# Routing stage of a two-layer diffusion transformer: which rows are transposed token-major, and where norm factor, scale and shift are applied

## The chip, the cores and the metric

The kernel runs on one core of one Trainium2 chip. The metric is the device time of one execution in microseconds (us). Five engines appear in the profile: PE (TensorE; PEld is its weight load), DVE (VectorE), ACT (ScalarE), POOL (GpSimd) and SP (SyncE), which here issues the loads of the weights.

## The reference, cut to what matters

256 tokens of width 1024 pass through two layers. The second layer ends in a mixture of experts; `norm_ffn_g`, `sc2` and `sh2` are rows of 1024.

```python
hl = rms_norm(xl, norm_ffn_g[1]) * (1 + sc2) + sh2     # rms_norm: x * rsqrt(mean(x*x) + eps) * g
xl = xl + g2 * moe_swiglu(hl, router, w1, w3, w2)

def moe_swiglu(h, router, w1, w3, w2):
    vals, idx = lax.top_k((h @ router).astype(jnp.float32), 2)
    wts = jax.nn.softmax(vals, axis=-1)
    combine = jnp.sum(jax.nn.one_hot(idx, 8) * wts[..., None], axis=-2)
    for e in range(8):
        y = y + combine[..., e:e + 1] * ((jax.nn.silu(h @ w1[e]) * (h @ w3[e])) @ w2[e])
```

With `A = (1 + sc2) * norm_ffn_g` per feature and `r` per token, a row of `hl` is `x * r * A + sh2`.

## The kernel before, in words

**Layout.** The residual lies feature-major: `xt[k]`, k from 0 to 7, holds features 128k to 128k+127 on its partitions and the 256 tokens in its first 256 columns; the other 256 columns are free by the routing stage. `r` lies token-major, two columns for two tiles of 128 tokens.

**Experts.** Only tokens that picked an expert are computed. For an expert, a one-hot matrix (token by slot) is multiplied with a token-major copy of the normed rows, `htok` (256 tokens by 1024), which yields `xg`: the expert's rows, feature-major, in up to 128 slots. Four experts ("large", positions 0, 2, 4, 6 of the list `SEQ`) run with 128 slots and an accurate product of three matmuls: `mm3` (L261 to L263) multiplies hi by hi, hi by lo and lo by hi, where hi is the rounded value and lo the remainder. The other four ("small") have 64 slots and one plain product; their rows are gathered at once by `gather_small` into the free half of `xt`. Expert 0 comes first; the order of the others is worked out on the chip from the counts (`order_a`), and SP loads the resulting indices into its registers (`order_load`, L1411) before it may issue any load of the other seven.

**Weights.** All weights come as pieces of 1 MB through ten buffers (`raw` and `q`, five each). For a large expert ACT makes hi of a piece (L233) and DVE lo (L211), into three pairs of hi and lo tiles, and the buffer is then free for the next load. Small experts multiply straight from the buffer. Large and small experts alternate in steps: hidden products (`eh`, `eh_small` L1538), transposes of the hidden rows (`et` L1558), output products (`ey`, `ey_small` L1595), and after an expert's last step `scatter` (L1618, L1622).

**Order.** Each engine works in the order in which the program names its instructions; nothing reorders them. A large expert's `gather` stands behind `ey` of the large expert before it (ACT L1581 and DVE L1582 scale its outputs) and behind the splitting of the next pieces. `xg` has one buffer.

**The routing stage.** `route_a` finishes the logits and the norm: `SumSq.finish` computes `r`, and two DVE instructions at L315 make `dg`, the identity times `r`. `route_b` then runs `bcast` (L320, a matmul that spreads `r` over partitions), the top-2 selection on DVE (L1308 to L1319), five products of the selection with a triangle or with ones (L1322 to L1326) for each token's slot (`rank`) and the counts, and then, for each k, DVE `xt[k] * r` (L1331) and ACT `* A + sh2` (L1333) into the free half. After the fourth k it puts rank, the first one-hots (L1428), counts and `order_a` (up to L1384) on DVE. Only behind the eighth k come 16 transposes on PE (L1347), four copies into `htok` (L1348, two on DVE, two on ACT), and `gather(0)`: 16 products (L1480, two matmul records each), and for each half of the features one ACT cast to hi (L1483) and one DVE subtraction for lo (L1484), both from PSUM.

Of the kernel before, what the change touches and what calls it, by code (L numbers as in the profile page):

```python
# [22 lines left out]
F32 = mybir.dt.float32  # L23
# [4 lines left out]
AF = mybir.ActivationFunctionType  # L28
ALU = mybir.AluOpType
AX = mybir.AxisListType  # L30

P = 128
D = 1024
KD = 8
T = 512
L = 256
FF = 3584
NFG = 7
E = 8
# [47 lines left out]
def build(ctx, tc, io):  # L87
    nc = tc.nc
    ve, se, te = nc.vector, nc.scalar, nc.tensor
# [3 lines left out]
    cp = ctx.enter_context(tc.tile_pool(name="cp", bufs=1))  # L93
# [4 lines left out]
    pools = {"s": phase.enter_context(tc.tile_pool(name="sp", bufs=SB, side="right"))}  # L98
# [4 lines left out]
    cnt = [0]  # L103
# [5 lines left out]
    def S(dtype=F32):  # L109
        return pools["s"].tile([P, 512], dtype, tag="s", name=nm("s"))  # L110
# [7 lines left out]
    def PS():  # L118
        return pp.tile([P, 512], F32, tag="p", name=nm("p"))
# [7 lines left out]
    f32 = lambda ap: ap.bitcast(F32)  # L127
# [3 lines left out]
    ident = cp.tile([P, P], F32, name="ident")  # L131
    xt = [xp.tile([P, 512], F32, tag="xt", name=f"xt{k}") for k in range(KD)]
# [3 lines left out]
    ones = cp.tile([P, P], F32, name="ones")  # L136
# [8 lines left out]
    Affn = [cp.tile([P, KD, 2], F32, name=f"af{l}") for l in range(2)]  # L145
    SH1, SC1, G1, SH2, SC2, G2 = (8 * i for i in range(6))

    def mod(l, c, s):
        q = mpos(c)
        return modT[l][:, q, s:s + 1]  # L150
# [126 lines left out]
    def rsqrt(v, n):  # L277
        y = tiny(n)
        for op in rsqrt_ops(v, n, y):
            op()  # L280
        return y

    class SumSq:
# [17 lines left out]
        def add(self, src):  # L301
            self.accum(self.square(src))

        def finish(self):

            nt = self.n // P
            ps = PS()
            for t in range(nt):
                te.matmul(ps[:, t:t + 1], lhsT=self.acc[:, t * P:(t + 1) * P], rhs=ones[:, 0:1], start=True, stop=True)
            v = tiny(nt)  # L310
            ve.tensor_scalar(v, ps[:, :nt], 1.0 / D, EPS, op0=ALU.mult, op1=ALU.add)
            self.r = rsqrt(v, nt)
            self.dg = S()
            for t in range(nt):
                ve.tensor_scalar(self.dg[:, t * P:(t + 1) * P], ident, self.r[:, t:t + 1], None, op0=ALU.mult)  # L315
# [11 lines left out]
    C = {}  # L327
# [964 lines left out]
    def route_a(_):  # L1292
        logits(6)
        logits(7)
        C["ss"].finish()

    def route_b(_):
        pb = C["ss"].bcast()
        r = C["ss"].r
        iota8 = iota[:, :E]  # L1300
        sel = cp.tile([P, 2, E], F32, name="sel")
        comb = cp.tile([P, 2, E], F32, name="comb")
        rank = cp.tile([P, 2, E], F32, name="rank")
        lgs = tiny(16).rearrange("p (t e) -> p t e", t=2)
        mx = tiny(16).rearrange("p (t e) -> p t e", t=2)
        ix = tiny(16, U32).rearrange("p (t e) -> p t e", t=2)
        for t in range(2):
            ve.scalar_tensor_tensor(lgs[:, t, :], C["lg"][t][:, :E], r[:, t:t + 1], C["c0"], op0=ALU.mult, op1=ALU.add)  # L1308
            ve.max(mx[:, t, :], lgs[:, t, :])
            ve.max_index(ix[:, t, :], mx[:, t, :], lgs[:, t, :])  # L1310
        del C["lg"]
        xf = tiny(4).rearrange("p (t c) -> p t c", t=2)
        ve.tensor_copy(xf, ix[:, :, 0:2])
        o0 = tiny(16).rearrange("p (t e) -> p t e", t=2)
        o1 = tiny(16).rearrange("p (t e) -> p t e", t=2)
        for t in range(2):
            ve.tensor_scalar(o0[:, t, :], iota8, xf[:, t, 0:1], None, op0=ALU.is_equal)
            ve.tensor_scalar(o1[:, t, :], iota8, xf[:, t, 1:2], None, op0=ALU.is_equal)
        ve.tensor_add(sel, o0, o1)  # L1319
        tri = cst[:, K_TRI:K_TRI + P]  # L1320
        ps = PS()
        te.matmul(ps[:, 0:E], lhsT=tri, rhs=sel[:, 0, :], start=True, stop=True)  # L1322
        te.matmul(ps[:, E:2 * E], lhsT=tri, rhs=sel[:, 1, :], start=True, stop=False)
        te.matmul(ps[:, E:2 * E], lhsT=ones, rhs=sel[:, 0, :], start=False, stop=True)
        te.matmul(ps[:, 2 * E:3 * E], lhsT=ones, rhs=sel[:, 0, :], start=True, stop=False)
        te.matmul(ps[:, 2 * E:3 * E], lhsT=ones, rhs=sel[:, 1, :], start=False, stop=True)  # L1326

        hn = []
        for k in range(KD):
            t = S()  # L1330
            ve.tensor_mul(t[:, :L], xt[k][:, :L], pb[:, :L])  # L1331
            hn.append(xt[k][:, L:])
            se.activation(hn[k], t[:, :L], AF.Identity, bias=mod(1, SH2 + k, 0), scale=Affn[1][:, k, 0:1])  # L1333
            if k == 3:
                ve.tensor_copy(rank, ps[:, 0:2 * E].rearrange("p (t e) -> p t e", t=2))
                C["sel"], C["comb"], C["rank"] = sel, comb, rank
                onehots(0)
                cnt = C["cnt"] = cp.tile([P, E], F32, name="cnt")
                ve.tensor_copy(cnt, ps[:, 2 * E:3 * E])
                order_a()  # L1340
                order_load()
        htok = C["htok"] = pools["t"].tile([P, 2, D], F32, tag="htok", name="htok")
        for hf in range(2):
            for t in range(2):
                pt = PS()
                for k in range(4):
                    te.transpose(pt[:, k * P:(k + 1) * P], hn[4 * hf + k][:, t * P:(t + 1) * P], ident)  # L1347
                (se.copy if t else ve.tensor_copy)(htok[:, t, hf * 512:(hf + 1) * 512], pt)  # L1348
        gather(0)
        flush_tails()  # L1350

        w = tiny(6).rearrange("p (c t) -> p c t", t=2)
        ve.tensor_sub(w[:, 0, :], mx[:, :, 1], mx[:, :, 0])
        se.activation(w[:, 0, :], w[:, 0, :], AF.Exp)
        ve.tensor_scalar(w[:, 1, :], w[:, 0, :], 1.0, None, op0=ALU.add)
        ve.reciprocal(w[:, 1, :], w[:, 1, :])
        ve.tensor_mul(w[:, 2, :], w[:, 0, :], w[:, 1, :])
        for t in range(2):
            ve.tensor_scalar(o0[:, t, :], o0[:, t, :], w[:, 1, t:t + 1], None, op0=ALU.mult)
            ve.scalar_tensor_tensor(comb[:, t, :], o1[:, t, :], w[:, 2, t:t + 1], o0[:, t, :], op0=ALU.mult, op1=ALU.add)  # L1360
# [48 lines left out]
    def order_load():  # L1409

        _, C["ex"] = nc.values_load_multi_w_load_instructions(  # L1411
            C["exi"][0:1, :], engines=[mybir.EngineType.SP], min_val=1, max_val=E - 1)
        state["stop"] = None
        issue_dma()
# [8 lines left out]
    def onehots(n):  # L1423

        sel, _, rank = column(n)
        oh = S()
        for t in range(2):
            ve.tensor_scalar(oh[:, t * P:(t + 1) * P], iota, rank(t), sel(t), op0=ALU.is_equal, op1=ALU.mult)  # L1428
        C["oh"] = [oh[:, t * P:(t + 1) * P] for t in range(2)]
# [41 lines left out]
    def gather(n):  # L1471

        oh = C.pop("oh")
        xg = pools["t"].tile([P, 2, KD, P], F32R, tag="xg", name=nm("xg"))
        for hf in range(2):
            ps = PS()
            for kk in range(4):
                k = 4 * hf + kk
                for t in range(2):
                    te.matmul(ps[:, kk * P:(kk + 1) * P], lhsT=C["htok"][:, t, k * P:(k + 1) * P], rhs=oh[t],  # L1480
                              start=(t == 0), stop=(t == 1), skip_group_check=True)
            pv = ps.rearrange("p (k c) -> p k c", k=4)
            se.copy(xg[:, 0, 4 * hf:4 * hf + 4, :], pv)  # L1483
            ve.tensor_sub(xg[:, 1, 4 * hf:4 * hf + 4, :], pv, f32(xg[:, 0, 4 * hf:4 * hf + 4, :]))  # L1484
        C["xg"] = [(xg[:, 0, k, :], xg[:, 1, k, :]) for k in range(KD)]

    def gather_small(_):

        oh = C.pop("ohs")
        for k in range(KD):  # L1490
            ps = PS()
            for t in range(2):
                te.matmul(ps[:, :L], lhsT=C["htok"][:, t, k * P:(k + 1) * P], rhs=oh[t], start=(t == 0), stop=(t == 1))
            se.copy(xt[k][:, L:], ps[:, :L])

    ada(1, 10, quiet=True, late=True)
    step(route_a, quiet=True)
# [220 lines left out]
    sel, comb, rank, htok = C["sel"], C["comb"], C["rank"], C["htok"]  # L1718
    with tc.If(cv > 0):
        for t in range(2):  # L1720
            ve.tensor_sub(rank[:, t, :], rank[:, t, :], C["slots"])
        with tc.For_i(0, E, 1) as ei:
# [11 lines left out]
            ps = PS()  # L1734
# [5 lines left out]
            for k in range(KD):  # L1740
                ps = PS()
                for t in range(2):
                    te.matmul(ps[:, :P], lhsT=htok[:, t, k * P:(k + 1) * P], rhs=oh[:, t * P:(t + 1) * P],
                              start=(t == 0), stop=(t == 1))
                ve.tensor_copy(xg[k // 4][:, (k % 4) * P:(k % 4 + 1) * P], ps[:, :P])
            yp = [PS(), PS()]
            for fg in range(NFG):
                hp = []
# [153 lines left out]
```

## Time and profile before

| | before |
|---|---|
| median of 3 runs | 1876.35 us (1871.52 to 1877.16) |
| profiled execution | 1877.55 us |
| its span, first to last instruction | 1875.8 us |
| mean granted TensorE clock | 0.987 |
| busy: PE, DVE, ACT, POOL | 95%, 61%, 41%, 24% |
| read from HBM | 487.32 MB |

The span is 1.75 us shorter than the profiled execution's own time. The routing stage lies at 975 to 997 us of the span; the experts follow and take the rest, about 880 us. A share of busy time is an average over stages; what a stage waits for has to be read from the stage itself. A PE share near 100% says that matmuls were in flight, not that the array did useful work at its peak.

### The profile page before, as it was taken

How to read it: one execution, taken by the hardware profiler on the slowest of the kernel's cores; microseconds unless marked ns; L12 is line 12 of the kernel's file. 1: busy time of each engine (PE TensorE's matmuls, PEld its weight loads, DVE VectorE, ACT ScalarE, POOL GpSimd, SP SyncE). 2: the span in 40 equal slices, each digit the busy share in tenths (PEclk: the TensorE clock that was granted, in tenths of full speed). 3: DMA queues.
4: the chain of work that ended last, by engine and by line, in shares of the span. 5: the costliest groups of instructions: out<-in, count | busy, mean ns of one | idle time of the engine just before them, and what ended most of it. 6: DMA issues, size and time to landing. Idle time of an engine off the chain costs nothing.

```text
span 1875.8 us, 24122 instructions
## 1 busy us (share of the span) xinstructions
PE 1790.5 (95%) x9438; PEld 1303.1 (69%) x9438; DVE 1136.1 (61%) x1645; ACT 772.5 (41%) x867; POOL 444.3 (24%) x189
## 2 busy tenths in 40 slices
PE   6999999999999999987999999999999999999997
PEld 4889877788888888876587656565656665656563
DVE  4888873488977421659758455555555655565553
ACT  4545543432222222245636444444444444444441
POOL 1677446244444443316500000000000000000000
PEclk9999999999999999988999999999999999999999
DMA  9432143554543422340076899999999999999995
GB/s 363 170 135 90 68 169 146 194 188 145 192 157 139 154 90 93 112 177 23 1 314 247 345 420 419 393 399 408 420 419 368 400 414 421 418 385 401 416 421 213
DMA packets 71686, 489.99 MB, mean 261 GB/s; under 512 B 8080, under 2 KB 9488, under 8 KB 13200
## 3 DMA queue, kind: packets, MB, share of 16 engines
q1 hardware_dynamic: 70992, 487.88, 65.8%
q8 instruction: 76, 1.25, 0.3%
q10 hardware_dynamic: 576, 0.52, 0.1%
q14 instruction: 42, 0.34, 0.1%
HBM read 487.32 MB, written 1.05 MB: 260 GB/s over the span
## 4 chain that ended last, share of the span: by engine, by line
PE 70%; DMA 12%; DVE 10%; ACT 4%; issue 3%; SPq 0%; POOL 0%; DVEq 0%; ACTq 0%; POOLq 0%
PE p L261 17%; PE p L263 17%; PE p L262 17%; DMA raw<-in_moe 8%; PE p L1538 8%; DVE lo L211 3%; DMA q<-in_moe 3%; ACT hi L233 2%; PE p L1595 2%; PE p L1161 2%; DVE p L568 1%; PE p L1558 1%; PE p L370 1%; PE p L1143 1%; DVE s L1523 1%
## 5 line engine op out<-in xcount | busy, mean ns | idle before, releaser
L211 POOL TENSOR_TENSOR lo<-raw,hi 128x2048 fp32r<-128x2048 f32 (+1 forms) x69 | 315.3, 4573 | 422.2 <-ACT hi L233 414.9
L233 ACT CAST hi<-raw 128x2048 fp32r<-128x2048 f32 x172 | 327.5, 1907 | 186.9 <-PE p L263 78.1
L261 PE MATMUL p<-s,hi 128*128 128x512 f32 x960 | 375.8, 391 | 0.7 <-ACT s L433 0.7
L262 PE MATMUL p<-s,hi 128*128 128x512 f32 x960 | 374.7, 390 | 1.4 <-DVE s L763 1.1
L263 PE MATMUL p<-s,lo 128*128 128x512 f32 x960 | 374.4, 390 | 0.6 <-POOL lo L205 0.6
L211 DVE TENSOR_TENSOR lo<-raw,hi 128x2048 fp32r<-128x2048 f32 (+1 forms) x107 | 244.7, 2289 | 79.1 <-ACT hi L233 79.1
L211 DVE TENSOR_TENSOR lo<-q,hi 128x2048 fp32r<-128x2048 f32 x70 | 160.2, 2292 | 215.3 <-ACT hi L233 213.5
L233 ACT CAST hi<-q 128x2048 fp32r<-128x2048 f32 x70 | 133.4, 1907 | 185.5 <-DMA q<-in_moe 133.0
L261 PEld LDWEIGHTS p<-s,hi 128*128 128x128 f32 x960 | 180.8, 188 | 39.9 <-ACT s L433 0.9
L262 PEld LDWEIGHTS p<-s,hi 128*128 128x128 f32 x960 | 180.6, 188 | 40.0 <-DVE s L763 1.7
L263 PEld LDWEIGHTS p<-s,lo 128*128 128x128 f32 x960 | 180.5, 188 | 38.7 <-POOL lo L205 1.1
L263 PE MATMUL p<-hi,xg 128*128 128x512 f32 x448 | 175.5, 392 | 5.4 <-DVE xg L1484 5.4
L261 PE MATMUL p<-hi,xg 128*128 128x512 f32 x448 | 179.2, 400 | 0.0
L262 PE MATMUL p<-lo,xg 128*128 128x512 f32 x448 | 175.8, 392 | 2.2 <-DVE lo L211 2.1
L262 PE MATMUL p<-lo,s 128*128 128x256 f32 (+1 forms) x480 | 161.0, 335 | 6.1 <-POOL lo L211 3.9
L261 PE MATMUL p<-hi,s 128*128 128x256 f32 (+1 forms) x480 | 164.3, 342 | 0.0
L396 DVE SCALAR_TENSOR_TENSOR s<-raw,o 128x512 f32<-128x512 f32 x128 | 158.9, 1302 | 0.0
L1538 PE MATMUL p<-q,xt 128*64 128x512 f32 x552 | 150.3, 602 | 0.0
L445 DVE SCALAR_TENSOR_TENSOR xt<-p,mod,xt 128x256 f32<-128x256 f32 x216 | 90.3, 475 | 76.9 <-PE p L263 69.5
L568 DVE SCALAR_TENSOR_TENSOR p<-s,vecs,p 128x494 f32<-128x494 f32 (+11 forms) x192 | 125.8, 732 | 6.1 <-ACT p L550 6.1
L263 PE MATMUL p<-hi,s 128*128 128x512 f32 (+1 forms) x352 | 123.6, 351 | 0.0
L261 PEld LDWEIGHTS p<-hi,s 128*128 128x128 f32 x480 | 92.0, 192 | 30.1 <-issue 21.9
(252 smaller groups left out, 2220.2 us busy)
## 6 DMA issues: line engine op xcount, KB each, us to landing
raw<-in_moe SPq DMA_DIRECT2D x181, 1024.0 KB, 10.2
q<-in_moe SPq DMA_DIRECT2D x153, 1024.0 KB, 14.1
raw<-in_ff SPq DMA_DIRECT2D x42, 1024.0 KB, 4.9
raw<-in_ada SPq DMA_DIRECT2D x31, 1024.0 KB, 6.4
raw<-in_adaT SPq DMA_DIRECT2D x16, 1024.0 KB, 4.8
raw<-in_w_ag SPq DMA_DIRECT2D x8, 1024.0 KB, 7.1
raw<-in_w_uv SPq DMA_DIRECT2D x8, 1024.0 KB, 4.9
raw<-in_w_out SPq DMA_DIRECT2D x6, 1024.0 KB, 5.0
```

Source lines behind the costliest of these rows:

```text
L211: eng.tensor_sub(lo[:, sl], r[:, sl], f32(hi[:, sl]))
L233: se.copy(hi, raws[i])
L261: te.matmul(out, lhsT=lh[0], rhs=rh[0], start=first, stop=False, skip_group_check=True)
L262: te.matmul(out, lhsT=lh[0], rhs=rh[1], start=False, stop=False, skip_group_check=True)
L263: te.matmul(out, lhsT=lh[1], rhs=rh[0], start=False, stop=last, skip_group_check=True)
L370: te.matmul(ps[32 * j:32 * j + 32, :P], lhsT=cpad[:, k, :], rhs=rv[:, kk, j * P:(j + 1) * P], start=(k == 0), stop=(k == 7), skip_group_ch ...
L396: ve.scalar_tensor_tensor(j, g[0][:, jj * D + q * 512:jj * D + (q + 1) * 512], 1.0, C["cb"][s][q], op0=ALU.mult, op1=ALU.mult, accum_out=h ...
L445: ve.scalar_tensor_tensor(xt[d][:, sl], ps[:, sl], mod(l, gbase + d, s), xt[d][:, sl], op0=ALU.mult, op1=ALU.add)
L568: ve.scalar_tensor_tensor(ov[:, :, lo:hi], gv[:, :, lo + s:hi + s], vecs[:, w0 + j:w0 + j + 1], ov[:, :, lo:hi], op0=ALU.mult, op1=ALU.add)
L1161: te.matmul(ps[HD * z:HD * z + HD, :L], lhsT=v, rhs=t[:, z, c, :], start=(c == 0), stop=(c == 3), skip_group_check=True, tile_position=(0, ...
L1538: te.matmul(ps[SMALL * z:SMALL * (z + 1), :], lhsT=xt[k][:, o:o + SMALL], rhs=w[z][:, kk, :], start=(k == 0), stop=(k == 7), skip_group_ch ...
L1595: te.matmul(yps[n][SMALL * z:SMALL * (z + 1), :], lhsT=hT[:, f * SMALL:(f + 1) * SMALL], rhs=w[:, ff, z * 512:(z + 1) * 512], start=(fg == ...
```

## The change

`finish` makes `dg` no longer for this norm, and `bcast` goes. The transposes take the raw residual and stand at the head of `route_b`, ahead of the selection; their four copies are all on ACT. The five products of the selection become four, in two PSUM tiles, and rank waits for the first two of them. `r` is multiplied into the selection (`selr`), so that the one-hots carry `r` in place of 1. The loop of L1331 and L1333 is gone. `A` and `sh2` are applied to the gathered rows: in `gather`, for each k, one ACT instruction (hi) and one DVE instruction into a new tile `v`, and for each half one subtraction `v - hi`; in `gather_small` and in the overflow loop, by the ACT instruction that copies from PSUM.

```diff
-        def finish(self):
+        def finish(self, diag=True):
...
             self.r = rsqrt(v, nt)
+            if not diag:
+                return
             self.dg = S()
...
-        C["ss"].finish()
+        C["ss"].finish(diag=False)
+
+    def modulated(o, ps, k):
+
+        se.activation(o, ps, AF.Identity, bias=mod(1, SH2 + k, 0), scale=Affn[1][:, k, 0:1])
...
     def route_b(_):
-        pb = C["ss"].bcast()
         r = C["ss"].r
+        htok = C["htok"] = pools["t"].tile([P, 2, D], F32, tag="htok", name="htok")
+        for hf in range(2):
+            for t in range(2):
+                pt = PS()
+                for k in range(4):
+                    te.transpose(pt[:, k * P:(k + 1) * P], xt[4 * hf + k][:, t * P:(t + 1) * P], ident)
+                se.copy(htok[:, t, hf * 512:(hf + 1) * 512], pt)
...
-        ps = PS()
-        te.matmul(ps[:, 0:E], lhsT=tri, rhs=sel[:, 0, :], start=True, stop=True)
-        te.matmul(ps[:, E:2 * E], lhsT=tri, rhs=sel[:, 1, :], start=True, stop=False)
-        te.matmul(ps[:, E:2 * E], lhsT=ones, rhs=sel[:, 0, :], start=False, stop=True)
-        te.matmul(ps[:, 2 * E:3 * E], lhsT=ones, rhs=sel[:, 0, :], start=True, stop=False)
-        te.matmul(ps[:, 2 * E:3 * E], lhsT=ones, rhs=sel[:, 1, :], start=False, stop=True)
-
-        hn = []
-        for k in range(KD):
-            t = S()
-            ve.tensor_mul(t[:, :L], xt[k][:, :L], pb[:, :L])
-            hn.append(xt[k][:, L:])
-            se.activation(hn[k], t[:, :L], AF.Identity, bias=mod(1, SH2 + k, 0), scale=Affn[1][:, k, 0:1])
-            if k == 3:
-                ve.tensor_copy(rank, ps[:, 0:2 * E].rearrange("p (t e) -> p t e", t=2))
-                C["sel"], C["comb"], C["rank"] = sel, comb, rank
-                onehots(0)
-                cnt = C["cnt"] = cp.tile([P, E], F32, name="cnt")
-                ve.tensor_copy(cnt, ps[:, 2 * E:3 * E])
-                order_a()
-                order_load()
-        htok = C["htok"] = pools["t"].tile([P, 2, D], F32, tag="htok", name="htok")
-        for hf in range(2):
-            for t in range(2):
-                pt = PS()
-                for k in range(4):
-                    te.transpose(pt[:, k * P:(k + 1) * P], hn[4 * hf + k][:, t * P:(t + 1) * P], ident)
-                (se.copy if t else ve.tensor_copy)(htok[:, t, hf * 512:(hf + 1) * 512], pt)
+        ps, pc = PS(), PS()
+        te.matmul(ps[:, 0:2 * E], lhsT=tri, rhs=sel.rearrange("p t e -> p (t e)"), start=True, stop=False,
+                  skip_group_check=True)
+        te.matmul(ps[:, E:2 * E], lhsT=ones, rhs=sel[:, 0, :], start=False, stop=True, skip_group_check=True)
+        te.matmul(pc[:, 0:E], lhsT=ones, rhs=sel[:, 0, :], start=True, stop=False)
+        te.matmul(pc[:, 0:E], lhsT=ones, rhs=sel[:, 1, :], start=False, stop=True)
+        for t in range(2):
+            ve.tensor_scalar(selr[:, t, :], sel[:, t, :], r[:, t:t + 1], None, op0=ALU.mult)
+        ve.tensor_copy(rank, ps[:, 0:2 * E].rearrange("p (t e) -> p t e", t=2))
+        C["sel"], C["comb"], C["rank"] = selr, comb, rank
+        onehots(0)
+        cnt = C["cnt"] = cp.tile([P, E], F32, name="cnt")
+        ve.tensor_copy(cnt, pc[:, 0:E])
+        order_a()
+        order_load()
         gather(0)
...
-            pv = ps.rearrange("p (k c) -> p k c", k=4)
-            se.copy(xg[:, 0, 4 * hf:4 * hf + 4, :], pv)
-            ve.tensor_sub(xg[:, 1, 4 * hf:4 * hf + 4, :], pv, f32(xg[:, 0, 4 * hf:4 * hf + 4, :]))
+            v = S()
+            for kk in range(4):
+                k, pk = 4 * hf + kk, ps[:, kk * P:(kk + 1) * P]
+                modulated(xg[:, 0, k, :], pk, k)
+                ve.tensor_scalar(v[:, kk * P:(kk + 1) * P], pk, Affn[1][:, k, 0:1], mod(1, SH2 + k, 0), op0=ALU.mult,
+                                 op1=ALU.add)
+            ve.tensor_sub(xg[:, 1, 4 * hf:4 * hf + 4, :], v.rearrange("p (k c) -> p k c", k=4),
+                          f32(xg[:, 0, 4 * hf:4 * hf + 4, :]))
...
-            se.copy(xt[k][:, L:], ps[:, :L])
+            modulated(xt[k][:, L:], ps[:, :L], k)
```

## Rows read from the trace of the kernel before

**Rows 1.** The page's span in 40 slices: busy tenths of PE and DMA
```profile
PE   6999999999999999987999999999999999999997
...
DMA  9432143554543422340076899999999999999995
```

**Rows 2.** Busy time by stretch (us, count), then clock, DMA share, GB/s: expert stage
```profile
1100.00:1190.00 90.00, 86.38 (x391) 52.66 (x390) 49.17 (x37) 40.78 (x31) 0.00 (x0) 1.00 1.01 420
1209.00:1225.00 16.00, 16.00 (x81) 7.88 (x81) 11.21 (x13) 5.39 (x5) 0.00 (x0) 1.00 0.74 281
```

**Rows 3.** The same view, two stretches behind the routing stage
```profile
998.00:1003.00 5.00, 4.90 (x22) 3.75 (x21) 4.50 (x7) 4.67 (x3) 0.00 (x0) 1.00 0.14 25
1030.00:1038.00 8.00, 8.00 (x39) 4.41 (x39) 0.86 (x1) 2.16 (x6) 0.00 (x0) 1.00 0.04 17
```

**Rows 4.** Waits of SP's queue, 960 to 1100 us: total, times, longest
```profile
SPq L1411 <- DVE s L1331: 10.4, 1, 10.4
```

**Rows 5.** Instructions in order of time, routing stage: start, us, engine, line
```profile
978.04 1.08 PE L370 MATMUL p<-q,cpad 128*32 128x128 f32 x32
...
979.45 0.48 DVE L315 TENSOR_SCALAR s<-ident,t 128x128 f32<-128x128 f32 x2
...
982.41 0.18 DVE L1319 TENSOR_TENSOR sel<-t,t 128x16 f32<-128x16 f32 x1
...
984.37 0.57 PE L1326 MATMUL p<-sel,ones 128*128 128x8 f32 x2
...
985.19 0.60 DVE L1428 TENSOR_SCALAR s<-cst,rank,sel 128x128 f32<-128x128 f32 x2
...
987.47 0.17 DVE L1384 CAST exi<-t 128x7 int32<-128x7 f32 x1
...
991.24 4.45 PE L1480 MATMUL p<-s,htok 128*128 128x128 f32 x32
...
996.35 0.69 DVE L1484 TENSOR_TENSOR xg<-p,xg 128x512 fp32r<-128x512 f32 x1 [1.09 <-ACT xg L1483]
...
997.32 3.70 ACT L233 CAST hi<-q 128x2048 fp32r<-128x2048 f32 x2
...
1014.18 0.60 PE L1558 MATMUL p<-ident,s 128*128 128x128 f32 x4
```

**Rows 6.** Instructions in order of time, the second large expert's gather; `gather_small`
```profile
1194.82 3.73 PE L1480 MATMUL p<-s,htok 128*128 128x128 f32 x32
...
1197.89 2.28 DVE L211 TENSOR_TENSOR lo<-raw,hi 128x2048 fp32r<-128x2048 f32 x1
...
1200.09 1.28 DVE L1484 TENSOR_TENSOR xg<-p,xg 128x512 fp32r<-128x512 f32 x2
...
1200.83 0.50 PE L263 MATMUL p<-hi,xg 128*128 128x512 f32 x1 [1.81 <-DVE xg L1484]
...
1026.43 7.07 PE L1493 MATMUL p<-s,htok 128*128 128x256 f32 x32
```

**Rows 7.** Groups by shape: busy us, mean ns, idle before: prices
```profile
L1462 DVE TENSOR_SCALAR s<-p 128x256 fp32r<-128x256 f32 x4 | 1.6, 412 | 0.0
L813 DVE TENSOR_TENSOR s<-s,s 128x512 fp32r<-128x512 f32 x8 | 5.4, 689 | 3.8 <-ACT s L808 2.0 <-PE p L262 1.8
...
L1333 ACT ACTIVATE xt<-s,mod,af 128x256 f32<-128x256 f32 x8 | 4.1, 588 | 6.4 <-DVE s L1331 6.4
L1348 ACT COPY htok<-p 128x512 f32<-128x512 f32 x2 | 1.1, 574 | 0.9 <-PE p L1347 0.9
```

**Rows 8.** Busy time by stretch as in rows 2, behind stalls of PE
```profile
983.00:984.00 1.00, 1.00 (x7) 1.00 (x6) 0.90 (x3) 1.00 (x3) 0.00 (x0) 0.50 1.00 426
1199.00:1203.00 4.00, 2.19 (x10) 1.80 (x10) 2.37 (x3) 0.18 (x1) 0.00 (x0) 1.00 1.01 418
1419.00:1423.00 4.00, 4.00 (x12) 3.15 (x11) 0.00 (x0) 1.20 (x1) 0.00 (x0) 0.57 1.03 426
1747.00:1751.00 4.00, 3.74 (x12) 1.63 (x14) 3.52 (x5) 0.59 (x1) 0.00 (x0) 0.57 1.01 418
```

More of the change, by code (lines that the diff above doesn't have):

```diff
@@ L1294, in route_a @@
         logits(7)
-        C["ss"].finish()
+        C["ss"].finish(diag=False)
+    def modulated(o, ps, k):
+        se.activation(o, ps, AF.Identity, bias=mod(1, SH2 + k, 0), scale=Affn[1][:, k, 0:1])
     def route_b(_):
-        pb = C["ss"].bcast()
         r = C["ss"].r
+        htok = C["htok"] = pools["t"].tile([P, 2, D], F32, tag="htok", name="htok")
[5 more added lines that the diff above has]
+                se.copy(htok[:, t, hf * 512:(hf + 1) * 512], pt)
         iota8 = iota[:, :E]
         sel = cp.tile([P, 2, E], F32, name="sel")
+        selr = cp.tile([P, 2, E], F32, name="selr")
         comb = cp.tile([P, 2, E], F32, name="comb")
@@ L1744, in build @@
                               start=(t == 0), stop=(t == 1))
-                ve.tensor_copy(xg[k // 4][:, (k % 4) * P:(k % 4 + 1) * P], ps[:, :P])
+                modulated(xg[k // 4][:, (k % 4) * P:(k % 4 + 1) * P], ps[:, :P], k)
             yp = [PS(), PS()]
```

## The prediction

> **What bounds the kernel now.** First the page's slices, 46.9 us each: PE is at nine tenths or more in most of them, and from the twenty-fourth on, in the experts, the DMA is too; in the two that hold the routing stage it is at 7 and 6 [rows 1]. The stage is then cut finer. Behind it the experts alternate. From 1100 to 1190 us the loads run at 420 GB/s without a break and PE is idle for 3.6 of 90 us; after a large expert has changed, PE is never idle for 16 us and the DMA stands at 0.74 [rows 2]. So neither engine sets the end alone: loads wait for buffers that PE's progress frees, and later PE waits for loads. A delay of PE at a change of expert delays the releases and comes back as idle DMA; I therefore pass it on to the end in full.
>
> What couples the routing stage to that? From 1030 to 1038 us the DMA is almost idle, 0.04, with PE busy throughout: all buffers are full and wait for PE. From 998 to 1003 us it was at 0.14 [rows 3]. The loads thus have spare time behind the stage, and it is PE's date, not theirs, that is handed on. SP's own wait, 10.4 us for the indices [rows 4], is long but covered.
>
> **Part 1, the path to the first gather.** The two instructions of `dg` take 0.48 us, whose end the next one overlaps, so 0.4 go; the selection ends at 982.19 in place of 982.59 [rows 5].
>
> The moved transposes issue 16 products on PE and four copies on ACT. PE is free from 979.12, where the last product of the ada step ends. Four transposes take 0.60 us at full clock [rows 5], 16 take 2.4: PE is done at 981.5, 0.7 before the selection needs it. ACT's four copies cost 4 x 0.574 = 2.3 us [rows 7] and run one behind PE, to about 982.1; no queue but these two is passed. If that cover went (half clock, 4.8 us), the products of the selection would start at 983.9 and everything after 1.7 us later.
>
> Before, the fifth product began at 984.37, 1.78 behind the selection, so they follow each other by 0.44; rank waits for the last, and the one-hots begin at 985.19, 2.6 behind the selection [rows 5]. Now two products lie ahead of rank, so three times 0.44, 1.3 us, go. The two small instructions for `selr` run on DVE while PE works. The one-hots begin at 982.19 + 1.3 = 983.5 and are ready at 984.1 in place of 985.79. The indices follow 1.85 us behind, at 985.95 in place of 987.64, so SP gains 1.7 us.
>
> The one-hots now find `htok` ready, so `gather(0)` starts its products at 984.4 in place of 991.24. The eight DVE and eight ACT instructions of the removed loop (the latter 588 ns each [rows 7]) were what it waited for. The products take 4.45 us as here or 3.73 as at the next gather [rows 5, 6]: end at 988.1 to 988.8 in place of 995.69. Then the second half's lo: before, the subtraction ended at 997.04, 1.35 us behind; now four instructions and a subtraction (part 2) take 2.0, so 990.1 to 990.8. That gives 6.2 to 6.9 us. The first ACT split behind it, at 997.32 [rows 5], and DVE's work shift by as much. **I take 6.5.** The added instructions of the first half lie beside the second half's products.
>
> **Part 2, the later gathers, three of them** (the pattern of rows 6 comes at 1194, 1412 and 1630 us). There PE is done with its products at 1198.55, but DVE finishes an unrelated split first, at 1200.17, and only then subtracts; PE waits 1.81 us for the first of two subtractions [rows 6]. DVE is on the path. Added ahead of that subtraction: four `tensor_scalar` of 128 columns from PSUM with two per-partition operands each. The trace has no such instruction. Nearest rows: 128 columns from SBUF with two such operands, two in 0.60 us [rows 5], thus 0.30 each; 256 columns from PSUM with constants, 412 ns [rows 7]. So 1.2 to 1.65 us for four. I take 0.34 each, 1.35 in all, nearer the first, which has the same operands. The subtraction itself now reads SBUF alone, 689 ns against 690 [rows 5, 7]: nothing. Three gathers: 3 x 1.35 = **4.05 us back**. The other half's subtraction, 2.0 us behind, is not late: PE has the twelve products of the first four k to do before it needs that, so nothing is added unless a product takes under 0.17. ACT's hi now takes four instructions per half; one costs at most 588 ns with 256 columns [rows 7], so 2.4 us a half, which ends before DVE's lo.
>
> By the Trainium skill, VectorE: DVE Perf Modes, section "Why PSUM operands drop a tier", a PSUM operand takes away the double rate that fp32 `tensor_scalar` has from SBUF. By that the four would cost 64 more cycles each than from SBUF, an estimate of 0.3 us in all at the page's 0.96 GHz, on top of 1.2: 1.5 and not 1.35.
>
> **Part 3, the clock.** A stall of PE has a second price. Of the three gathers with a stall of 1.8 us, the one at 1412 us was followed by a mean granted clock of 0.57 over 4 us, the one at 1194 us by none [rows 6, 8], and so was that at 1630. A wait of 2.3 us ahead of 1747 us was followed by 0.57 again [rows 8]. In the routing stage PE paused too, and at 983 us it was at 0.50, the 1.2 GHz level [rows 8]. The changed gathers stall for 1.8 + 1.35 = 3.2 us, so I expect the fall at all three. One fall costs at most 4 x 0.43 = 1.7 us; where it begins inside the stall, less, so 1.5. Three at 1.5 less the one of 1.7 that is there now: **2.8 us more**.
>
> [...]
>
> Edits at nothing: `gather_small`'s ACT instruction (588 ns for 256 columns in place of a copy) lies under 0.88 us of PE per k, 7.07 us for eight [rows 6]; without that cover 8 x 0.6 = 4.7 us at most. The overflow loop is only entered if a count exceeds its slots.
>
> **Sum.** -6.5 + 4.05 + 2.8 = +0.35 us on the profiled 1877.55. That execution is 1.2 above the median, so I put the sum on the median: 1876.35 + 0.35 = **1876.7 us**. With the ends of each term: -6.9 + 3.6 + 0 to -6.2 + 4.95 + 3.4, that is 1873 to 1878.5.
>
> **Rivals.**
> - No more falls of the clock. For it: the 1.81 us stall at 1194 passed without one. Then -6.5 + 4.05 = -2.45, 1873.9 us, still within what can be measured. Chance 0.15.
> - The late gathers' cost is hidden. If PE at 1200 us runs behind loads that have not come, a later PE loses nothing; the DMA is busy at 1.01 there [rows 8], which speaks for it. Against it: from 1209 to 1225 it falls to 0.74 with PE full [rows 2]. Then -6.5, 1869.85 us, faster. Chance 0.13.
> - Slower: the loads take the place of PE as what the start hands on. If SP's restart sets the date of the steps after 1000 us, only its 1.7 us are gained; with dearer DVE instructions (4.95) and three falls (3.4 more) the sum is +6.65, 1883.0 us. It decides if the DMA has no idle stretch left before the steady part; the 8 us at 0.04 [rows 3] speak against it. Chance 0.08.
> - The change doesn't do what it says: the raw transposes come late (PSUM tiles taken, or half clock) and hold the selection back. Then 1.7 us less, 1878.4. Chance 0.04.
>
> **Numbers.** The forecast has 0.60. A measurement of this kernel can tell about 0.3%, 5.6 us, from no change. Faster by more: the hidden case, 0.13. Slower by more: 0.08. The rest, 0.79, within. The range takes in the ends of the sum and the hidden case, and reaches about halfway from its upper end to the slower one: 1869.5 to 1880.5.
>
> **What would show it.** Right: `gather(0)` begins near 984.4, its lo ends near 990.5; the indices' last step ends near 986; the idle DMA stretch behind the stage is still there, some 6 us earlier; at the three later gathers the wait for the subtraction is near 3.2 us, with the clock at half behind it. Wrong: a wait there that stayed at 1.8, PE's start less than 5 us earlier, or a DMA that never idles between the stage and its steady part.

## The result, and the profile after

The changed kernel takes 1905.94 us (median of 4, 1904.07 to 1910.78); the kernel before, run beside it, 1876.67 (1871.52 to 1877.16). The ratio is 1.0159, with a 95% interval of 1.0142 to 1.0177: 29 us slower, where 1876.7 was forecast. The profiled execution took 1910.78 us, the longest of the four, its span 1908.9 against 1875.8. Two rows of its page's slices [rows 1]:

```profile
PE   6999999999999999987998999899998999899997
...
DMA  9432153544444322340076999899998999989995
```

Slices at 8 have appeared among the experts: PE loses time there. But the largest loss lies ahead of everything that the diff edits. Up to line 1295 the code of the two kernels is the same, two lines lower after the change. These are products of layer 0, at the first two of the three lines of `mm3`, in the list of costliest groups (busy us, mean ns of one), before:

```profile
L261 PE MATMUL p<-s,hi 128*128 128x512 f32 x960 | 375.8, 391 | 0.7 <-ACT s L433 0.7
L262 PE MATMUL p<-s,hi 128*128 128x512 f32 x960 | 374.7, 390 | 1.4 <-DVE s L763 1.1
```

and after:

```profile
L261 PE MATMUL p<-s,hi 128*128 128x512 f32 x960 | 381.6, 398 | 0.7 <-ACT s L435 0.7
L262 PE MATMUL p<-s,hi 128*128 128x512 f32 x960 | 380.6, 397 | 0.7 <-DVE s L765 0.5
```

Seven ns of 391 look like nothing, and the products overlap, so the mean isn't their price. The price is the distance of two starts, in order of time (start us, duration). Before:

```profile
400.37 0.39 PE L261 MATMUL p<-s,hi 128*128 128x512 f32 x1
400.60 0.39 PE L262 MATMUL p<-s,hi 128*128 128x512 f32 x1
400.82 0.39 PE L263 MATMUL p<-s,lo 128*128 128x512 f32 x1
401.05 0.39 PE L261 MATMUL p<-s,hi 128*128 128x512 f32 x1
```

After:

```profile
400.06 0.39 PE L261 MATMUL p<-s,hi 128*128 128x512 f32 x1
400.29 0.40 PE L262 MATMUL p<-s,hi 128*128 128x512 f32 x1
400.52 0.39 PE L263 MATMUL p<-s,lo 128*128 128x512 f32 x1
400.75 0.40 PE L261 MATMUL p<-s,hi 128*128 128x512 f32 x1
```

Three products take 0.68 us before and 0.69 to 0.70 after; over more than 1,200 of them between 400 and 700 us the mean distance is 0.2267 and 0.2333 us. There are 3 x 960 of these products: 2880 x 0.0067 = 19 us if all of it reached the end. It is the same engine, shape and code, and the granted clock is 1.00 there in both.

Then the routing stage, in order of time [rows 5]:

```profile
992.31 1.08 PE L372 MATMUL p<-q,cpad 128*32 128x128 f32 x32
993.32 1.97 PE L1310 MATMUL p<-ident,xt 128*128 128x128 f32 x16
994.07 2.05 ACT L1311 COPY htok<-p 128x512 f32<-128x512 f32 x4 [0.35 <-PE p L1310]
996.29 0.18 DVE L1332 TENSOR_TENSOR sel<-t,t 128x16 f32<-128x16 f32 x1
997.44 0.60 DVE L1428 TENSOR_SCALAR s<-cst,rank,selr 128x128 f32<-128x128 f32 x2
997.94 5.47 PE L1480 MATMUL p<-s,htok 128*128 128x128 f32 x32 [0.30 <-DVE s L1428]
999.72 0.17 DVE L1384 CAST exi<-t 128x7 int32<-128x7 f32 x1
...
1005.29 0.69 DVE L1488 TENSOR_TENSOR xg<-s,xg 128x512 fp32r<-128x512 f32 x1
...
1009.15 0.69 DVE L1488 TENSOR_TENSOR xg<-s,xg 128x512 fp32r<-128x512 f32 x1
...
1010.13 5.49 ACT L233 CAST hi<-q 128x2048 fp32r<-128x2048 f32 x3
...
1046.27 3.65 PE L1543 MATMUL p<-q,xt 128*64 128x512 f32 x16
```

The stage begins at 992.31 in place of 978.04: 14.27 us are gone by then. Taken from there, the gather's products start 7.6 us earlier than before (997.94 less 14.27 is 983.67, against 991.24), yet the second half's lo ends at 1009.84, which is 995.57, against 997.04: of the 7.6, 1.5 are left. The first product of the small experts is at 1046.27, 12.84 later than before: 1.4 gained. Before:

```profile
1033.43 3.65 PE L1538 MATMUL p<-q,xt 128*64 128x512 f32 x16
```

A late gather, the second large expert's [rows 6], shows where they went, for the same instructions run in the stage above:

```profile
1216.22 0.40 DVE L1486 TENSOR_SCALAR s<-p,af,mod 128x128 f32<-128x128 f32 x1
...
1216.66 0.46 ACT L1301 ACTIVATE xg<-p,mod,af 128x128 fp32r<-128x128 f32 x1 [2.64 <-DVE s L1486]
1217.15 0.41 DVE L1486 TENSOR_SCALAR s<-p,af,mod 128x128 f32<-128x128 f32 x1 [0.53 <-ACT xg L1301]
1217.60 0.46 ACT L1301 ACTIVATE xg<-p,mod,af 128x128 fp32r<-128x128 f32 x1 [0.48 <-DVE s L1486]
1218.09 0.41 DVE L1486 TENSOR_SCALAR s<-p,af,mod 128x128 f32<-128x128 f32 x1 [0.53 <-ACT xg L1301]
...
1219.47 0.69 DVE L1488 TENSOR_TENSOR xg<-s,xg 128x512 fp32r<-128x512 f32 x1
...
1220.22 0.80 PE L263 MATMUL p<-hi,xg 128*128 128x512 f32 x1 [5.03 <-DVE xg L1488]
```

Read the brackets: ACT was idle until DVE's instruction was done, DVE until ACT's. Neither needs the other's result. Both read the same PSUM tile, and take turns: 0.94 us for a block of 128 columns. PE's wait for the subtraction is 5.03 us where it was 1.81, at each of the three late gathers.

Last, the clock. Stretches of 4 us (PE, PEld, DVE, ACT, POOL busy; then granted clock, DMA share, GB/s) behind a late gather, behind two other stalls of PE, and two behind the routing stage [rows 3]:

```profile
1222.00:1226.00 4.00, 4.00 (x16) 3.18 (x15) 1.46 (x3) 2.08 (x2) 0.00 (x0) 0.81 0.87 363
1172.00:1176.00 4.00, 4.00 (x12) 1.10 (x10) 0.83 (x2) 0.00 (x0) 0.00 (x0) 0.54 1.01 420
1334.00:1338.00 4.00, 4.00 (x13) 1.20 (x13) 2.61 (x4) 0.59 (x1) 0.00 (x0) 0.50 1.01 420
1010.00:1015.00 5.00, 3.29 (x14) 2.40 (x15) 4.18 (x9) 4.98 (x4) 0.00 (x0) 1.00 0.00 0
1044.00:1052.00 8.00, 8.00 (x39) 3.82 (x39) 0.69 (x1) 2.63 (x5) 0.00 (x0) 1.00 0.11 22
```

Cut into stretches of 10 us from 1010 us to the end of the span, with 2 x (1 - clock) x 10 us of each counted as half clock, the expert stage has 12.6 us at half clock before and 33.6 after. Half of the difference, 10.5 us, is lost if PE sets the pace in it. So the spans' difference of 33.1 us comes out as 14.3 (ahead of the stage) - 1.4 (left of the gain) + 3 x 3.22 (late gathers) + 10.5 (clock) = 33.1. The term of the clock is an estimate, the others are read from the two traces.

### The profile page after: what moved, and what is told of

It is laid out like the page before. It is cut to its first block, busy times and chain, and to the rows that moved or that the text cites. A ratio compares the mean times of both kernels' runs of the same rounds, so it can differ in the third digit from the quotient of the medians.

```text
span 1908.9 us, 24153 instructions
## 1 busy us (share of the span) xinstructions
PE 1815.7 (95%) x9434; PEld 1304.8 (68%) x9434; DVE 1131.8 (59%) x1667; ACT 780.1 (41%) x885; POOL 444.4 (23%) x189
## 4 chain that ended last, share of the span: by engine, by line
PE 73%; DMA 11%; DVE 9%; ACT 4%; issue 2%; SPq 0%; POOL 0%; DVEq 0%; ACTq 0%
PE p L261 18%; PE p L263 18%; PE p L262 18%; PE p L1543 8%; DMA raw<-in_moe 7%; DVE lo L211 3%; PE p L1600 3%; DMA q<-in_moe 2%; ACT hi L233 2%; PE p L1163 2%; DMA raw<-in_ada 1%; PE p L372 1%; DVE p L570 1%; PE p L1563 1%; PE p L1145 1%
## 5 line engine op out<-in xcount | busy, mean ns | idle before, releaser
L261 PE MATMUL p<-s,hi 128*128 128x512 f32 x960 | 381.6, 398 | 0.7 <-ACT s L435 0.7
L262 PE MATMUL p<-s,hi 128*128 128x512 f32 x960 | 380.6, 397 | 0.7 <-DVE s L765 0.5
L263 PE MATMUL p<-s,lo 128*128 128x512 f32 x960 | 380.0, 396 | 0.6 <-POOL lo L205 0.6
L261 PEld LDWEIGHTS p<-s,hi 128*128 128x128 f32 x960 | 180.9, 188 | 45.1 <-ACT s L435 0.9
L261 PE MATMUL p<-hi,xg 128*128 128x512 f32 x448 | 180.1, 402 | 0.0
L261 PE MATMUL p<-hi,s 128*128 128x256 f32 (+1 forms) x480 | 164.7, 343 | 0.0
L1543 PE MATMUL p<-q,xt 128*64 128x512 f32 x552 | 156.0, 624 | 0.0
L398 DVE SCALAR_TENSOR_TENSOR s<-raw,o 128x512 f32<-128x512 f32 x128 | 145.7, 1200 | 0.0
L261 PEld LDWEIGHTS p<-hi,s 128*128 128x128 f32 x480 | 91.8, 191 | 29.9 <-issue 22.2
```

Source lines behind the costliest of these rows:

```text
L261: te.matmul(out, lhsT=lh[0], rhs=rh[0], start=first, stop=False, skip_group_check=True)
L262: te.matmul(out, lhsT=lh[0], rhs=rh[1], start=False, stop=False, skip_group_check=True)
L263: te.matmul(out, lhsT=lh[1], rhs=rh[0], start=False, stop=last, skip_group_check=True)
L398: ve.scalar_tensor_tensor(j, g[0][:, jj * D + q * 512:jj * D + (q + 1) * 512], 1.0, C["cb"][s][q], op0=ALU.mult, op1=ALU.mult, accum_out=h ...
L1543: te.matmul(ps[SMALL * z:SMALL * (z + 1), :], lhsT=xt[k][:, o:o + SMALL], rhs=w[z][:, kk, :], start=(k == 0), stop=(k == 7), skip_group_ch ...
```

## The experiments

The expectations call A the theory that the new `selr` tile is to blame for layer 0: it takes 64 bytes of every partition in the left part of SBUF and moves all tiles behind it, `hi` and `lo` among them, while `s` on the right side stays. C is the theory of the turns. Rivals are named in each.

**e1_layout** takes the tile away: `sel` goes into an existing scratch tile, so that all addresses are those of before.

```diff
-        sel = cp.tile([P, 2, E], F32, name="sel")
+        sel = tiny(16).rearrange("p (t e) -> p t e", t=2)
```

> The changed kernel, with the selection in one of the rotating small tiles in place of a tile of its own, so that every tile that lies behind it in SBUF is 64 bytes lower, where it was in the kernel before. Theory A (addresses): the products of layer 0 that load their weights from hi and lo tiles follow each other every 0.2334 us in the changed kernel and every 0.2267 before because those tiles lie 64 bytes higher; here they are back at 0.2267, the routing stage is about 14 us earlier and the time is near 1891 us. Rival B (the slower products come from the loads, the clock or the chip in that execution): 0.2334 stays or comes and goes, time near 1906.

Measured 1891.48 us, ratio 1.0064 (1.0041 to 1.0086), products 0.2267 us apart, the stall at the late gathers still 5.1:

```profile
1205.63 0.79 PE L263 MATMUL p<-hi,xg 128*128 128x512 f32 x1 [5.07 <-DVE xg L1488]
```

The routing stage begins at 982.20, which is 10.1 us earlier than in the changed kernel and not 14. The changed computation is not what slows layer 0.

**e2_pad64** is the kernel before with an unused tile of the same size, and nothing else.

```diff
+        cp.tile([P, 2, E], F32, name="pad")
```

> The kernel before, with an unused tile of 64 bytes per partition among the constants, nothing else. Theory A (addresses): products of layer 0 every 0.2334 us, the routing stage 14 us later, time near 1891 us, ratio to the kernel before near 1.0075. Rival B: 0.2267, 1876.7 us, ratio 1.000.

1891.8 us, 1.007 (1.0049 to 1.0092), mean distance 0.2333 to 0.2335 us by stretch of 100 us:

```profile
L261 PE MATMUL p<-s,hi 128*128 128x512 f32 x960 | 382.5, 398 | 0.7 <-ACT s L433 0.7
```

An unused tile costs 0.7%: A holds from both sides.

**e3_four** leaves the layout and ends the turns: all four ACT instructions stand ahead of the four of DVE.

```diff
             for kk in range(4):
+                modulated(xg[:, 0, 4 * hf + kk, :], ps[:, kk * P:(kk + 1) * P], 4 * hf + kk)
+            for kk in range(4):
                 k, pk = 4 * hf + kk, ps[:, kk * P:(kk + 1) * P]
-                modulated(xg[:, 0, k, :], pk, k)
                 ve.tensor_scalar(v[:, kk * P:(kk + 1) * P], pk, Affn[1][:, k, 0:1], mod(1, SH2 + k, 0), op0=ALU.mult,
```

> The changed kernel, with the four ACT instructions of a half ahead of the four DVE instructions in place of one by one. Theory C (turns): ACT and DVE wait for each other at every feature block because both read the same PSUM tile in turns, 0.94 us a block, and that makes PE's wait at a late gather 5.0 us in place of 1.8; with one turn per half the wait is 3.2 us, as four DVE instructions of 0.33 us make it, so 3 x 1.8 = 5.5 us less, and the first gather's lo some 2 us earlier: near 1899 us. Rival D (the four DVE instructions themselves take 0.94 us with PSUM, whoever else reads): the wait stays near 5.0 us and the time near 1906.

1895.91 us, 1.0098 (1.0069 to 1.0128). A late gather in its trace, in order of time:

```profile
1207.73 1.36 DVE L1487 TENSOR_SCALAR s<-p,af,mod 128x128 f32<-128x128 f32 x4
1209.12 0.69 DVE L1489 TENSOR_TENSOR xg<-s,xg 128x512 fp32r<-128x512 f32 x1
1209.73 1.36 DVE L1487 TENSOR_SCALAR s<-p,af,mod 128x128 f32<-128x128 f32 x4
1209.87 0.50 PE L263 MATMUL p<-hi,xg 128*128 128x512 f32 x1 [3.17 <-DVE xg L1489]
```

With no turns the four take 1.36 us and the wait is 3.17: the same instructions in another order of issue. C holds. The median fell by 10.0 us where about 7 were forecast; the four runs lie 10 us apart.

**e4_both** has both edits.

> Both edits, the lower addresses and four ACT ahead of four DVE instructions. If theories A and C hold and add up: 1906 - 14 - 7 = about 1885 us; as the prediction's sum has it, which knew of neither, 1876.7. If the clock still falls at every late gather the upper value is nearer, at fewer of them the lower. If B and D hold: 1906.

1879.89 us (10 runs), 1.0014 (1.0000 to 1.0028). The change as the prediction thought of it costs next to nothing, and gains nothing. The expectation had put it near 1885 if the clock fell at all three late gathers; it did fall at all three, and the time is 5 us less.

**e5_pad_both and e6_pad_right** ask what about the addresses counts. The kernel before, with 64 unused bytes on the left and on the right, and on the right alone (tiles there grow down from the end, so `s` moves down).

```diff
+    rp = ctx.enter_context(tc.tile_pool(name="rp", bufs=1, side="right"))
+    rp.tile([P, 16], F32, name="rpad")
...
+        cp.tile([P, 16], F32, name="pad")
```

> The kernel before, with unused tiles of 64 bytes on both sides of SBUF: the hi and lo tiles of the weights lie 64 bytes higher, the small tiles s that hold the activations 64 bytes lower, so their distance changes by 128 bytes. Theory A1 (what counts is the distance of the two operands' addresses, in steps of 128 bytes): the products of layer 0 stay at 0.2267 us and the time at that of the kernel before. Theory A2 (what counts is the address of hi and lo itself): 0.2334 us and 14 us more, ratio 1.0075.

> The kernel before, with the unused 64 bytes on the right side alone: hi and lo stay where they are, the s tiles lie 64 bytes lower. Theory A1 (distance): 0.2334 us in layer 0, 14 us more, ratio 1.0075. Theory A2 (the address of hi and lo): 0.2267 and no change.

1889.26 us, 1.0065 (1.0041 to 1.0089), and 1892.48, 1.0087 (1.0063 to 1.011). Both slow: neither the position of `hi` alone nor the distance modulo 128 bytes is it. In the next four, A1 and A2 stand for other theories than in e5 and e6, as each text says. They are the kernel before with other pads, one execution each:

> The kernel before with 128 unused bytes per partition ahead of hi (hi at 101984, s unmoved). Theory A1 (it is the position of each operand within 128 bytes that counts): nothing has changed, the layer's products p<-s,hi follow each other by 0.2267 us, the run is at 1877. Theory A2 (any move of hi or of the tiles beside it slows them): 0.233 us, some 1890.

> The kernel before with 128 unused bytes on either side (hi 101984, s 153440). Theory A1: 0.2267 us, 1877. Theory A2: 0.233 us, some 1890.

> The kernel before with both operands at a multiple of 128 bytes (hi 101888, s 153472). Theory A3 (an operand that lies 64 bytes off its old place within 128 is slow, one at 32 too): 0.233 us or more, some 1890. Theory A4 (a multiple of 128 is at least as good as before): at most 0.2267 us, 1877 or less.

> The kernel before with 32 unused bytes ahead of hi (hi at 101888, a multiple of 128, s unmoved at 153568). Theory A1: hi's position has changed, so 0.23 us or more, some 1885 to 1892. Theory A4 (only a position 64 bytes off is slow): 0.2267 us, 1877.

1894.21, 1877.06, 1885.37 and 1889.9 us; the kernel before, run once beside them, took 1883.65, so the rows decide and not these times. The group of L261 in e8:

```profile
L261 PE MATMUL p<-s,hi 128*128 128x512 f32 x960 | 381.1, 397 | 0.7 <-ACT s L433 0.7
```

The same in e9, where it stands two lines lower:

```profile
L263 PE MATMUL p<-s,hi 128*128 128x512 f32 x960 | 376.0, 392 | 0.7 <-ACT s L435 0.7
```

A1 fails in e8, A2 in e9, A4 in e10 and e11; A3 is left. All of them fit another reading as well (addresses as the built programs have them, bytes in a partition):

| kernel | hi | s | distance | modulo 256 | mean ns |
|---|---|---|---|---|---|
| before | 101856 | 153568 | 51712 | 0 | 391 |
| changed, e2 | 101920 | 153568 | 51648 | 192 | 398 |
| e6 | 101856 | 153504 | 51648 | 192 | 398 |
| e5 | 101920 | 153504 | 51584 | 128 | 396 |
| e8 | 101984 | 153568 | 51584 | 128 | 397 |
| e10 | 101888 | 153472 | 51584 | 128 | 397 |
| e11 | 101888 | 153568 | 51680 | 224 | 397 |
| e9 | 101984 | 153440 | 51456 | 0 | 392 |

That was formed behind the data, so **e12_dist** puts it to the test: the changed kernel with 192 bytes on the right. Both operands then lie elsewhere than before, at a distance that is a multiple of 256.

```diff
+    rp = ctx.enter_context(tc.tile_pool(name="rp", bufs=1, side="right"))
+    rp.tile([P, 48], F32, name="rpad")
```

> The changed kernel, nothing taken out, with 192 unused bytes per partition on the right side: s goes down to 153376, hi stays at 101920, so their distance is 51456 bytes, a multiple of 256 again, while neither lies where it was. Theory A5 (it is the distance of the two operands, modulo 256 bytes, that counts): the products p<-s,hi follow each other by 0.2267 us, layer 0 ends some 14 us earlier than in the changed kernel, the run is at about 1891 to 1893 as in e1_layout. Theory A2 (any move slows them) or A1 (each operand's own position): 0.232 to 0.234 us, 1904 to 1907.

1891.57 us, 1.0065 (1.0044 to 1.0087), 0.2267 us apart, and the routing stage begins at 977.22:

```profile
L263 PE MATMUL p<-s,hi 128*128 128x512 f32 x960 | 375.8, 391 | 0.7 <-ACT s L437 0.7
...
977.22 1.08 PE L374 MATMUL p<-q,cpad 128*32 128x128 f32 x32
```

More unused bytes won back what 64 had cost. A5 holds here, and A3 fails: `hi` lies 64 bytes off its old place within 128, and nothing is slower. Over all the traces, the routing stage begins at 975.3 to 982.2 us in the six programs with remainder 0 and at 988.8 to 998.2 us in the eight others, so the addresses part the two groups, while the size of their cost, 14 us, is known to a few us. The experts' products fit it too: `hi` and `xg` both moved in the changed kernel, their distance stayed, and their 0.2277 us became 0.2278. Why the distance counts is not shown. Nor is it shown that only the two operands of one product matter: the 96 products `p<-o,hi` that stand between those of layer 0 have both tiles on the left, where e6 moves nothing, and yet within each three of them the mean distance is 0.2298 us in e6 and 0.2265 before. All tiles on the left that lie behind the pad move together, so no run tells `hi` from the others there.

**e7_rows** keeps the early transposes and gives up part 2. The scale is applied feature-major as the residual is finished, `r` and the shift token-major, on DVE for features 0 to 511 and on ACT and GpSimd for the rest. One-hots and both gathers are those of before.

```diff
+                se.activation(xt[d][:, L:], xt[d][:, :L], AF.Copy, scale=Affn[1][:, d, 0:1])
...
+            se.activation(h, pts[2 + t], AF.Copy, scale=r[:, t:t + 1])
+            nc.gpsimd.tensor_tensor(h, h, shb[1], op=ALU.add)
...
+            ve.scalar_tensor_tensor(htok[:, t, :512], pts[t], r[:, t:t + 1], shb[0], op0=ALU.mult, op1=ALU.add)
```

> A third version, at the addresses of the kernel before: the residual is scaled by A on ACT in the steps before the routing stage and transposed early; r and the shift are applied token-major to the transposed rows (half of them by DVE, half by ACT and GpSimd), so that gather, gather_small and the one-hots are those of the kernel before. If the prediction's part 1 holds and its parts 2 and 3 were what took the gain back: the first gather starts some 6.5 us earlier, the late gathers wait 1.8 us as before, and the time is 6 us less than the kernel before, ratio 0.997. Rival (the early start is swallowed by loads that come later in the chain): ratio 1.000 with the first gather as early.

1873.75 us (12 runs), 0.9985 (0.9969 to 1.0000): the fastest of the three versions, halfway between the forecast (0.997) and the rival (1.000), and just at the edge of what 12 runs tell apart. From its order of time:

```profile
976.78 1.08 PE L372 MATMUL p<-q,cpad 128*32 128x128 f32 x32
...
984.32 3.62 PE L1491 MATMUL p<-s,htok 128*128 128x128 f32 x30 [1.33 <-DVE htok L1322]
...
988.60 0.69 DVE L1495 TENSOR_TENSOR xg<-p,xg 128x512 fp32r<-128x512 f32 x1 [1.09 <-ACT xg L1494]
...
1018.67 7.07 PE L1504 MATMUL p<-s,htok 128*128 128x256 f32 x32
```

`gather_small` is at 1018.67 in place of 1026.43 [rows 6], of which 1.26 were there when the stage began: 6.5 us come from the stage, what part 1 was taken for. The wait at the late gathers is 1.8 again. At half clock it has 19.1 us, 6.5 more than before, so some 3.2 go back by the same estimate; its span is 3.7 below. Why the clock fell for longer is open.

## Why the prediction was wrong

**The sum left out the new tile.** Of `selr` it said only that its two small instructions run on DVE while PE works. A tile has an address as well, and this one moved the operands of 2880 products outside the diff: 14.3 us in the profiled pair, 14.5 between the medians of the changed kernel and e1. Without it the change would still have been some 15 us slower (e1, 1891.48), outside the range; the parts below are the rest. No rival had it: each began at the routing stage. The chance of slower, 0.08, was put on the loads, and those were not it: the DMA still stands idle behind the stage, at 0.00 and 0.11.

**Part 2, the turns.** The step was "ACT's hi now takes four instructions per half [...] 2.4 us a half, which ends before DVE's lo" and 1.35 us for DVE's four. It treated the two engines as independent. The price was right (four in 1.36 us, e3; the wait 3.17 against 3.2 forecast), but in the order of the program they go in turns: 3.22 us more at each gather instead of 1.35. The Trainium skill, PSUM — Partial Sum Buffer, section "PSUM bank collisions raise a hardware error", says that two engines may not access the same partitions of one bank at the same time, reads included, and that such pairs are to be guarded by semaphores. The trace agrees: the idle time of each engine ends with the other's read, 0.53 us for DVE and 0.48 for ACT at each block. No run gave each engine a tile of its own, so that the shared tile makes them wait is argued from the code; that the order of the reads sets the price is shown by e3. That is the rule that spoke against this change, and it wasn't weighed. The one that was weighed, on the rate of a PSUM operand, gave an estimate of 1.5 us; the row says 1.36.

**Part 1.** The path to the gather was right. Less the 14.27, the one-hots begin at 983.17 (forecast 983.5), the products at 983.67 (984.4), the indices are ready at 985.62 (985.95), and SP's wait for them is 7.4 us [rows 4]. The cover held: 16 transposes in 1.97 us, all ACT copies done before the selection. The products took 5.47 us, with a granted clock of 0.55 to 0.59 from 998 to 1002 us, where 3.73 to 4.45 were taken. Wrong was the sentence "the added instructions of the first half lie beside the second half's products". Less the 14.27, the first half's lo ends at 991.7, behind the products, and the second half's at 995.6 in place of 990.1 to 990.8. Without the turns (e4, whose stage begins 2.71 earlier than before) DVE starts on the second half at 988.23, when the first is done, and ends at 990.31: with 2.71 added 993.0, so 4.0 us gained and not 6.5:

```profile
988.23 1.36 DVE L1487 TENSOR_SCALAR s<-p,af,mod 128x128 f32<-128x128 f32 x4
...
989.62 0.69 DVE L1489 TENSOR_TENSOR xg<-s,xg 128x512 fp32r<-128x512 f32 x1
```

The clock is part of that: e4's products took 5.41 us, at a granted clock of 0.50 from 981 to 983 us. In e3 they took 3.84 at 1.00, and the same lo ends at 1004.44; its stage begins 13.05 later than before, so 5.6 are gained.

**Part 3.** Falls of the clock were forecast at all three late gathers, and e4 has all three, 3.4 to 6.8 us at half clock. By size it fell short: in the changed kernel three more came behind other stalls, of 2.68 to 2.96 us, while the kernel before has a stall of 2.64 there without one. They make 17 us at half clock, so some 8.6 lost. Nothing in the sum stood for them, and no run here settles what brought them on; the length of the stall alone doesn't, for in e3 one of 2.90 us passed without a fall and one of 1.95 was followed by 0.59.

For e4 the sum without the first two errors comes out, and not quite by its terms: -4.0 + 3 x 1.41 + (23.3 - 12.6)/2 = +5.6, with -2.7 from the layer ahead of it +2.9, against +2.3 measured between the spans. The forecast of next to nothing thus holds for this version by terms that differ from the forecast's and cancel, which is in part luck.

## What to carry to other kernels

Before an edit is costed at nothing, ask what it allocates: compare the addresses of all operands of the longest loop in the two built programs, and look at that loop in both traces first, although the diff doesn't touch it. Where two engines read one PSUM tile, let each do all of its reads at a stretch, or (not tried here) give each a tile of its own; in turns, a block of 128 columns cost the sum of both, 0.94 us. A path that was shortened by 7 us pays only as far as the next engine on it is free.

## What the runs showed of the hardware that was not expected

Products of 128x128 by 128x512 (fp32r) follow each other every 0.2267 us where the two operands' addresses in a partition differ by a multiple of 256 bytes, and every 0.232 to 0.234 us at remainders of 128, 192 and 224, at all the positions of the operands that were tried; the products `p<-s,hi` of all 14 programs run here fit, one of them foretold. It is 2.5 to 3%, at full granted clock, and shows in no wait. Down in the experts the products `p<-hi,s` go the same way: 0.2279 us before, 0.2293 at 192, 0.2324 at 128 (e8) and 0.2281 at 0 (e9). Products `p<-hi,s` of 256 columns don't: their median distance is 0.120 us before and 0.118 in the changed kernel.
